# Weight sums on VectorE, a gate stage that stays in PSUM, and a last norm shared by three engines

## The chip, the core and the metric

The kernel runs on one core of one Trainium2 chip. TensorE (PE; its weight loads are PEld) multiplies from SBUF into PSUM, VectorE (DVE), ScalarE (ACT) and GpSimd (POOL) work on tiles in SBUF and PSUM, SyncE (SP) issues the DMA transfers. Every engine works through its own instructions in a fixed order and waits where an operand is not there. The metric is the device time of one execution in microseconds; lower is better.

## The reference

One layer of a hybrid encoder, for 1024 tokens of width 1024, in fp32:

```
x = LN1(alpha*x + 0.5*SwiGLU_1(x))
x = LN2(alpha*x + W_o[ RMS(FoX(x)) || RMS(ShortConv(x)) ])
x = LN3(alpha*x + 0.5*SwiGLU_2(x))
x = LN4(alpha*x + sigmoid(x W_g + b_g) * (p W_p))

SwiGLU(x): gate, up = split(x @ w_in);  return (silu(gate) * up) @ w_out     # hidden width 2816
```

The change touches the output product `... @ w_out` of both SwiGLU blocks and the last line (the gate stage).

## The kernel before

**Precision.** An fp32 product is made from three matmuls of a reduced format: each operand is split into a hi part (a copy by ScalarE, line 123) and a lo part (source minus hi, by VectorE, line 124; both inputs lie in SBUF), and `mm3` (lines 142 to 144) adds hi·hi, lo·hi and hi·lo in PSUM. A block of weights of 128x512 passes through rings of seven hi tiles (`wh`) and seven lo tiles (`wl`); six tiles take loads from HBM (`raw`) and five are for intermediates (`tmp`). There are eight PSUM banks of 128x512.

**Output product (`ffn_out`, called once for each FFN).** The product of hidden activations and w_out is made by a scheme of Strassen and Winograd with seven products of half-size blocks. Each product n = 0 to 6 has eleven steps j; a step splits one tile of hidden activations (`H`, loaded from `h_d`) and one block of weights, and issues 4 token tiles x 3 matmuls of 512 columns. The weights are: b11 (n = 0), t3 = b22 - b12 (n = 1), t2 = t3 + b11, formed in place (n = 2), t4 (n = 3), t1 (n = 4), b21 (n = 5), b22 (n = 6). t3, t2, t4 and t1 are sums of two blocks that GpSimd forms (lines 137 and 417; 44 sums in each FFN). After a product, four banks are evicted into the row tiles `r0` to `r7` by VectorE (line 467: `r += 0.5*ps`); so the residual must be in `r` before. `rest` loads the residual, a quarter (four tiles of 128x512) during each of products 0 to 3, and ScalarE (FFN 1, line 523) or GpSimd (FFN 2, line 976, times the gains) scales it. In FFN 2 a row of biases is added by a matmul with a one-step contraction (line 465: 33 rows, `ones_k`). Rows r0 to r3 are normalised in product 5, r4 to r7 at the end of product 6 (`norm`: statistics on VectorE, the power -0.5 on GpSimd at line 223, the scaling on VectorE).

**Gate stage.** It follows FFN 2 without a break: w_g is split block by block (`w_block`), and the first half of the tokens is multiplied with it for both halves n of the columns; the rows r4 to r7 are transposed (line 207) between the steps. `affine` turns the normalised rows into the residual of the last line (times a gain, plus a bias, on GpSimd, lines 1055 and 1056; 16 operations for four rows). `gate` finishes a bank: bias on VectorE from a broadcast row (line 1028), sigmoid on ScalarE (line 1029), times the projected embedding on GpSimd (line 1030; on VectorE for the last two), and the sum with `r` on VectorE (line 1031), then statistics (line 1036). `finish_out` is the last norm of a row: statistics, power on GpSimd (line 1043), and two operations for each half row on VectorE:

```
        stt = nc.vector.scalar_tensor_tensor
        for n in range(2):
            o = r[t][:, half(n)]
            stt(o, o, mv[:, 0:1], gb4[n], op0=sub, op1=mult)
            stt(o, o, rs, gb4[2 + n], op0=mult, op1=add)
            nc.sync.dma_start(out[tok(t), half(n)], o)
```

**Order.** The kernel is written in a tile framework: its scheduler decides, from its own estimates of time, where an instruction stands on its engine, except where `keep_in_program_order` or, in the change, `issue_after` (not ahead of a given instruction) binds it.

Of the kernel before, what the change touches and what calls it, by code (L numbers as in the profile page):

```python
# [8 lines left out]
F32 = mybir.dt.float32  # L9
# [9 lines left out]
P = 128  # L19
# [6 lines left out]
H = 8  # L26
# [25 lines left out]
def kernel(ctx: ExitStack, tc: tile.TileContext, x, xT, pT, f1_in, f1_out, f2_in,  # L52
# [247 lines left out]
    def ffn_in(w_in, get, early, wait, free, first=None):  # L300
# [77 lines left out]
        up.release()  # L378

    def ffn_out(w_out, init, after0, after1, extra=None):  # L380

# [15 lines left out]
        def h_load(n, j):  # L397
# [41 lines left out]
        for n, (_, get_w, b, (i, nn)) in enumerate(prods):  # L439
# [539 lines left out]
    def row_pair(o, n):  # L979


        a = [temp() for _ in range(n + 1)]
        for i, t in enumerate(a):
            nc.vector.memset(t[0:33], 0.0)
            for q in (0, 32):
                nc.sync.dma_start(t[q:q + 1], rows[3:4, half(i)])
        if n:
            nc.vector.tensor_tensor(a[1][0:33], a[1][0:33], a[0][0:33], op=sub)
        t, l = a[n], temp()
        nc.vector.tensor_scalar(t[0:33], t[0:33], 2 * ALPHA, None, op0=mult)  # L990
        nc.scalar.copy(o[0:33], t[0:33])
# [4 lines left out]
    def after0(r):  # L996
# [25 lines left out]

    def gate(hf, t, ps, c0, w=HB, eng=nc.gpsimd):
# [144 lines left out]
```

## Time and profile before

| | |
|---|---|
| three runs, us | 1951.53, 1954.69, 1953.48 (median 1953.48) |
| profiled execution, us | 1955.81 |
| its span, from the first to the last instruction, us | 1954.0 |
| mean granted TensorE clock | 0.985 |
| busy: TensorE, VectorE, GpSimd, ScalarE | 1874.5, 1442.4, 997.6, 799.8 us |
| FFN 1's output product, about | 442 to 655 us |
| FFN 2's output product, about | 1611 to 1844 us |
| gate stage and end, about | 1815 to 1954 us |

Windows give, for a stretch of time, the busy time of each engine in the order PE, PEld, DVE, ACT, POOL with the number of instructions that started, then TensorE's granted clock as a share of full speed, the share of time in which the DMA engines were busy, and GB/s. Waits name an engine and a line, and after the arrow the instruction whose end released it. Matmuls overlap, so a matmul's listed duration is longer than its share of TensorE's time; the pieces of the chain show that share.

### The profile page before, as it was taken

The numbers are of one execution on the slowest core, as the hardware profiler recorded it, in microseconds if no ns is written. First come the engines' busy times: TensorE is split into PE (matmuls) and PEld (weight loads), VectorE is DVE, ScalarE is ACT, GpSimd is POOL, SyncE is SP. The second block draws the span as 40 slices with busy tenths as digits, with TensorE's granted clock in tenths as the row PEclk, the third lists the DMA queues.
The fourth block names the chain that finished last, engine by engine and source line by source line (L and its number), as shares of the span: only waits on it lengthen the run. The fifth ranks groups of instructions, "written<-read, shape, count | busy, mean of one in ns | idle before, by whom it ended". The sixth has DMA issues, their size and how long they took to land.

```text
span 1954.0 us, 25776 instructions
## 1 busy us (share of the span) xinstructions
PE 1874.5 (96%) x8632; PEld 1540.8 (79%) x8632; DVE 1442.4 (74%) x1999; ACT 799.8 (41%) x1420; POOL 997.6 (51%) x725
## 2 busy tenths in 40 slices
PE   8799999999999989999899999999999999899896
PEld 7688888888788868887688778888888887688685
DVE  7966555548767689976988877976555568987968
ACT  5322333325444553444665526433333334344430
POOL 2787566545550154431841322697565546850673
PEclk9899999999999999999999999999999999999998
DMA  7454323239555533378963123455332249554312
GB/s 238 150 185 163 117 102 119 96 121 379 171 186 178 183 115 119 105 253 273 267 172 91 56 91 118 146 194 178 105 124 93 97 139 365 186 189 152 123 59 98
DMA packets 167938, 307.60 MB, mean 157 GB/s; under 512 B 18503, under 2 KB 26951, under 8 KB 167805
## 3 DMA queue, kind: packets, MB, share of 16 engines
q1 hardware_dynamic: 167804, 305.95, 46.4%
q8 instruction: 68, 1.11, 0.2%
q14 instruction: 66, 0.53, 0.1%
HBM read 221.93 MB, written 83.95 MB: 157 GB/s over the span
## 4 chain that ended last, share of the span: by engine, by line
PE 76%; DVE 12%; issue 5%; DMA 3%; POOL 2%; ACT 1%; SPq 0%; DVEq 0%; ACTq 0%; POOLq 0%
PE ps L143 23%; PE ps L144 22%; PE ps L142 22%; DVE wl L124 4%; DVE tt L137 1%; PE pt L830 1%; PE pt L142 1%; PE pt L143 1%; PE pt L144 1%; PE ps_s L785 1%; PE po L838 1%; PE ps_s L782 1%; DVE S L124 1%; DVE pr L792 1%; PE po L837 1%
## 5 line engine op out<-in xcount | busy, mean ns | idle before, releaser
L142 PE MATMUL ps<-S,wh 128*128 128x512 f32 x896 | 350.8, 392 | 14.0 <-ACT S L123 6.5
L143 PE MATMUL ps<-S,wh 128*128 128x512 f32 x896 | 350.8, 392 | 4.0 <-DVE S L124 4.0
L144 PE MATMUL ps<-S,wl 128*128 128x512 f32 x896 | 350.2, 391 | 0.4 <-DVE wl L124 0.4
L123 ACT CAST wh<-tmp 128x512 fp32r<-128x512 f32 x268 | 164.7, 621 | 355.7 <-PE ps L143 268.5
L124 DVE TENSOR_TENSOR wl<-tmp,wh 128x512 fp32r<-128x512 f32 x268 | 256.8, 959 | 32.4 <-ACT wh L123 32.2
L143 PE MATMUL ps<-wl,wh 128*128 128x512 f32 x616 | 243.3, 395 | 15.1 <-DVE wl L124 15.1
L124 DVE TENSOR_TENSOR wl<-raw,wh 128x512 fp32r<-128x512 f32 x231 | 200.1, 870 | 75.7 <-ACT wh L123 75.4
L123 ACT CAST wh<-raw 128x512 fp32r<-128x512 f32 x239 | 146.6, 621 | 261.7 <-PE ps L143 208.3
L137 POOL TENSOR_TENSOR tmp<-raw 128x512 f32<-128x512 f32 x112 | 159.9, 1428 | 165.2 <-DVE wl L124 106.0
L144 PE MATMUL ps<-wh,wl 128*128 128x512 f32 x616 | 241.1, 391 | 0.0
L142 PE MATMUL ps<-wh 128*128 128x512 f32 x616 | 226.4, 393 | 0.7 <-ACT wh L123 0.7
L137 POOL TENSOR_TENSOR tmp<-raw,tmp 128x512 f32<-128x512 f32 x112 | 158.0, 1411 | 114.4 <-DVE wl L124 54.3
L142 PEld LDWEIGHTS ps<-S,wh 128*128 128x128 f32 x896 | 169.1, 189 | 50.5 <-ACT S L123 7.3
L143 PEld LDWEIGHTS ps<-S,wh 128*128 128x128 f32 x896 | 169.2, 189 | 40.5 <-DVE S L124 5.7
L144 PEld LDWEIGHTS ps<-S,wl 128*128 128x128 f32 x896 | 169.2, 189 | 36.2 <-DVE wl L124 1.1
L343 POOL TENSOR_TENSOR c<-c,sil 128x512 f32<-128x512 f32 x78 | 124.0, 1591 | 74.2 <-DVE c L250 43.3
L143 PEld LDWEIGHTS ps<-wl,wh 128*128 128x128 f32 x616 | 116.2, 189 | 45.8 <-DVE wl L124 22.2
L124 DVE TENSOR_TENSOR wl<-H,wh 128x512 fp32r<-128x512 f32 x154 | 147.4, 957 | 2.3 <-ACT wh L123 2.2
L142 PEld LDWEIGHTS ps<-wh 128*128 128x128 f32 x616 | 115.5, 188 | 25.8 <-ACT wh L123 1.8
L144 PEld LDWEIGHTS ps<-wh,wl 128*128 128x128 f32 x616 | 116.3, 189 | 23.5
L137 POOL TENSOR_TENSOR c<-c 128x512 f32<-128x512 f32 x88 | 128.1, 1460 | 6.7 <-DMA c<-e_d 1.9
L262 DVE TENSOR_TENSOR u<-ps,u 128x512 f32<-128x512 f32 x136 | 92.0, 683 | 47.2 <-PE ps L144 47.1
(299 smaller groups left out, 3988.0 us busy)
## 6 DMA issues: line engine op xcount, KB each, us to landing
raw<-in_f_in SPq DMA_DIRECT2D x216, 256.0 KB
h_d<-c SPq DMA_DIRECT2D x154, 256.0 KB
H<-h_d SPq DMA_DIRECT2D x154, 256.0 KB
raw<-in_f_out SPq DMA_DIRECT2D x132, 256.0 KB
z_d<-r SPq DMA_DIRECT2D x16, 512.0 KB
raw<-in_w_conv_in SPq DMA_DIRECT2D x32, 256.0 KB
r<-z_d SPq DMA_DIRECT2D x32, 256.0 KB
s_d<-s SPq DMA_DIRECT2D x28, 256.0 KB
```

The costliest lines, as they stand in the source:

```text
L123: nc.scalar.copy(h, src)
L124: (eng or nc.vector).tensor_tensor(l, src, h.bitcast(F32), op=sub)
L137: eng.tensor_tensor(t, a, b, op=op)
L142: mm(ps, a[0], b[0], start=first, stop=False, skip_group_check=onto)
L143: mm(ps, a[0], b[1], start=False, stop=False, skip_group_check=onto)
L144: mm(ps, a[1], b[0], start=False, stop=last, skip_group_check=onto)
L262: nc.vector.tensor_tensor(o, ps, u, op=add)
L343: nc.gpsimd.tensor_tensor(c, c, sil.pop((j, i, hf)), op=mult)
L782: mm(st[:, b:b + n], q["QA"][:, tok(t)], q["KA"][:, b:b + n], start=True, stop=False)
L785: mm(st[:, b:b + n], q["QB"][:, tok(t)], q["KB"][:, b:b + n], start=False, stop=True)
L792: nc.vector.tensor_scalar(pr[:, 0:w], pr[:, 0:w], l, None, op0=mult)
L830: nc.tensor.transpose(pv[:, j, t, :], prs[t][:, tok(2 * jp + j)], ident)
```

## The change

1. The sums t3, t2, t4 and t1 go from GpSimd to VectorE. t2, t4 and t1 may not stand ahead of the lo part of the block five steps on in the product before (`done`).
2. The first product's banks are evicted by ScalarE as `r = 0.5*ps`, without a residual. The residual's quarters come in products 1 to 4 in another order; the quarter (1, 0), which comes last, is loaded into a `tmp` tile and added to `r` (FFN 1: one operation on VectorE; FFN 2: a multiplication and an addition on GpSimd, so GpSimd has 20 operations there instead of 16).
3. In `gate`, the bias is a one-step matmul into the bank; sigmoid (ScalarE) and the multiplication (VectorE) work in PSUM, and VectorE adds `r`. The bank is free only after that sum. `row_pair` now also prepares the bias rows.
4. In `finish_out`, ScalarE normalises, VectorE multiplies by the gain, and GpSimd adds the bias (VectorE for the last row).
5. `affine(0)` stands behind the power of the last `norm` on GpSimd.

```diff
     def put(h, l, src, eng=None):
         nc.scalar.copy(h, src)
-        (eng or nc.vector).tensor_tensor(l, src, h.bitcast(F32), op=sub)
+        return (eng or nc.vector).tensor_tensor(l, src, h.bitcast(F32), op=sub)
...
+        def sums(n, j, o, a, b, op):
+            with tc.issue_after(done[n - 1, min(j + 5, NP - 1)]):
+                nc.vector.tensor_tensor(o, a, b, op=op)
+            return o
...
         def w_t3(j):
             b22, b12 = load(w_out[j + NP][:, half(1)]), load(w_out[j][:, half(1)])
-            return tt(nc.gpsimd, b22, b12, sub, lambda: ztile(NP + j))
+            return tt(nc.vector, b22, b12, sub, lambda: ztile(NP + j))
 
         def w_t2(j):
             t = ztile(NP + j)
-            tc.keep_in_program_order(nc.gpsimd.tensor_tensor(t, t, ztile(j), op=add))
-            return t
+            return sums(2, j, t, t, ztile(j), add)
 
         def w_t4(j):
-            return tt(nc.gpsimd, load(w_out[j + NP][:, half(0)]), ztile(NP + j), sub)
+            return sums(3, j, temp(), load(w_out[j + NP][:, half(0)]), ztile(NP + j), sub)
...
-                if n < 4 and j in (1, 3, 5, 7):
+                if n > 0 and n < 5 and j in (1, 3, 5, 7):
                     next(late_init)
...
-                nc.vector.scalar_tensor_tensor(rs, ps[t], 0.5, rs, op0=mult, op1=add)
+                if n == 0:
+                    nc.scalar.activation(rs, ps[t], AF.Copy, scale=0.5)
+                else:
+                    nc.vector.scalar_tensor_tensor(rs, ps[t], 0.5, rs, op0=mult, op1=add)
                 if n == 6:
-                    norm(r[4 + t])
+                    last_norm[0] = norm(r[4 + t])
...
-        for i, nn in ((1, 0), (0, 1), (0, 0), (1, 1)):
+        for i, nn in ((0, 1), (0, 0), (1, 1), (1, 0)):
             for t in range(4 * i, 4 * i + 4):
                 o = r[t][:, half(nn)]
-                tc.keep_in_program_order(nc.sync.dma_start(o, src[tok(t), half(nn)]))
-                yield o, nn
+                z = temp() if (i, nn) == (1, 0) else o
+                tc.keep_in_program_order(nc.sync.dma_start(z, src[tok(t), half(nn)]))
+                yield z, o, nn
...
-        for o, n in rest(r, z_d[1]):
-            tc.keep_in_program_order(nc.gpsimd.tensor_tensor(o, o, gains[n], op=mult))
+        for z, o, n in rest(r, z_d[1]):
+            tc.keep_in_program_order(nc.gpsimd.tensor_tensor(z, z, gains[n], op=mult))
+            if z is not o:
+                tc.keep_in_program_order(nc.gpsimd.tensor_tensor(o, o, z, op=add))
             yield
...
-        pl, c = load(ple_d[tok(row), cs]), temp((P, w))
-        nc.vector.tensor_tensor(c, ps, bg[:, cs], op=add)
-        nc.scalar.activation(c, c, AF.Sigmoid)
-        eng.tensor_tensor(c, c, pl, op=mult)
-        nc.vector.tensor_tensor(r[row][:, cs], r[row][:, cs], c, op=add)
+        pl = load(ple_d[tok(row), cs])
+        mm(ps, ones_k, bg[c0 // HB][:, c0 % HB:c0 % HB + w], start=False, stop=True,
+           skip_group_check=True)
+        nc.scalar.activation(ps, ps, AF.Sigmoid)
+        nc.vector.tensor_tensor(ps, ps, pl, op=mult)
+        nc.vector.tensor_tensor(r[row][:, cs], ps, r[row][:, cs], op=add)
...
-        stt = nc.vector.scalar_tensor_tensor
+        off = small.tile([P, 1], F32, name="off", tag="off")
+        nc.vector.scalar_tensor_tensor(off, mv[:, 0:1], -1.0, rs, op0=mult, op1=mult)
         for n in range(2):
             o = r[t][:, half(n)]
-            stt(o, o, mv[:, 0:1], gb4[n], op0=sub, op1=mult)
-            stt(o, o, rs, gb4[2 + n], op0=mult, op1=add)
+            nc.scalar.activation(o, o, AF.Identity, bias=off, scale=rs)
+            nc.vector.tensor_tensor(o, o, gb4[n], op=mult)
+            eng.tensor_tensor(o, o, gb4[2 + n], op=add)
             nc.sync.dma_start(out[tok(t), half(n)], o)
...
-    affine(0)
+    with tc.issue_after(last_norm[0]):
+        affine(0)
...
     for t in outs:
-        finish_out(t)
+        finish_out(t, nc.vector)
```

**Where instructions stand.** On VectorE, in product 1 of FFN 2, before: lo parts of `H` and of the weights t3 (`T`) take turns.

```order
L124 TENSOR_TENSOR wl_15988<-H_15755,wh_15987 128x512
L124 TENSOR_TENSOR wl_15998<-T_15995,wh_15997 128x512
L124 TENSOR_TENSOR wl_16017<-H_15755,wh_16016 128x512
L124 TENSOR_TENSOR wl_16026<-T_15995,wh_16025 128x512
L124 TENSOR_TENSOR wl_16044<-H_15817,wh_16043 128x512
L124 TENSOR_TENSOR wl_16054<-T_16051,wh_16053 128x512
```

The same place in the change:

```order
L137 TENSOR_TENSOR T_15993<-raw_15989,raw_15991 128x512
L124 TENSOR_TENSOR wl_15932<-T_15937,wh_15931 128x512
L414 TENSOR_TENSOR T_15755<-T_15755,T_15525 128x512
L137 TENSOR_TENSOR T_15993<-raw_16018,raw_16020 128x512
L124 TENSOR_TENSOR wl_15957<-H_15701,wh_15956 128x512
L124 TENSOR_TENSOR wl_15961<-T_15937,wh_15960 128x512
L414 TENSOR_TENSOR T_15821<-T_15821,T_15525 128x512
L124 TENSOR_TENSOR wl_15984<-H_15747,wh_15983 128x512
L137 TENSOR_TENSOR T_16049<-raw_16045,raw_16047 128x512
L124 TENSOR_TENSOR wl_15988<-T_15993,wh_15987 128x512
```

Between the lo parts now stand sums t3 (line 137), which need two loads (`raw`), some steps ahead of their use, and sums t2 for the next product (line 414).

On GpSimd, around the last norm of FFN 2, before (`rs` is the power of `norm`; `gb` the gain and the bias of `affine`):

```order
L137 TENSOR_TENSOR tmp<-raw,T 128x512 x14
L223 TENSOR_TENSOR rs<-rs,mhalf 128x1 x4
L1055 TENSOR_TENSOR r_15489<-r_15489,gb_17608 128x512
L1055 TENSOR_TENSOR r_15490<-r_15490,gb_17608 128x512
...
L1056 TENSOR_TENSOR r_15491<-r_15491,gb_17608 128x512
L1056 TENSOR_TENSOR r_15492<-r_15492,gb_17608 128x512
L223 TENSOR_TENSOR rs<-rs,mhalf 128x1 x4
```

And in the change:

```order
L995 TENSOR_TENSOR tmp<-tmp,gains 128x512
L997 TENSOR_TENSOR r_15500<-r_15500,tmp 128x512
L223 TENSOR_TENSOR rs<-rs,mhalf 128x1 x8
L1081 TENSOR_TENSOR r_15493<-r_15493,gb_17620 128x512
L1081 TENSOR_TENSOR r_15494<-r_15494,gb_17620 128x512
...
L1082 TENSOR_TENSOR r_15493<-r_15493,gb_17620 128x512
L1082 TENSOR_TENSOR r_15494<-r_15494,gb_17620 128x512
```

The sums t4 and t1 (`tmp<-raw,T`) are gone, and the 16 operations of `affine(0)` stand behind all eight powers; all eight multiplications now come ahead of the eight additions.

On VectorE, the end of the program before (`r_15495` and `r_15496` are the last two rows):

```order
L1047 SCALAR_TENSOR_TENSOR r_15495<-r_15495,mv,gb 128x512 x2
L1030 TENSOR_TENSOR tmp<-tmp,raw 128x256
L1048 SCALAR_TENSOR_TENSOR r_15495<-r_15495,rs,gb 128x512 x2
L1031 TENSOR_TENSOR r_15496<-r_15496,tmp 128x256
L1036 BN_STATS st_18248<-r_15496 128x6
L1040 BN_AGGR mv<-st_18248 128x2
L1042 TENSOR_SCALAR rs<-mv 128x1
L1047 SCALAR_TENSOR_TENSOR r_15496<-r_15496,mv,gb 128x512 x2
L1048 SCALAR_TENSOR_TENSOR r_15496<-r_15496,rs,gb 128x512 x2
```

And in the change (the same rows are `r_15499` and `r_15500`):

```order
L1069 SCALAR_TENSOR_TENSOR off<-mv,rs 128x1
L1073 TENSOR_TENSOR r_15499<-r_15499,gb 128x512 x2
L1054 TENSOR_TENSOR ps<-ps,raw 128x256
L1055 TENSOR_TENSOR r_15500<-ps,r_15500 128x256
L1060 BN_STATS st_18271<-r_15500 128x6
L1064 BN_AGGR mv<-st_18271 128x2
L1066 TENSOR_SCALAR rs<-mv 128x1
L1069 SCALAR_TENSOR_TENSOR off<-mv,rs 128x1
L1073 TENSOR_TENSOR r_15500<-r_15500,gb 128x512 x2
L1074 TENSOR_TENSOR r_15500<-r_15500,gb 128x512 x2
```

Ahead of the last row's product, VectorE now has two multiplications of the row before instead of four operations.

## Rows read from the trace of the kernel before

**Rows 1.** The page: busy time by engine (1), and the chain by engine (4).
```profile
PE 1874.5 (96%) x8632; PEld 1540.8 (79%) x8632; DVE 1442.4 (74%) x1999; ACT 799.8 (41%) x1420; POOL 997.6 (51%) x725
...
PE 76%; DVE 12%; issue 5%; DMA 3%; POOL 2%; ACT 1%; SPq 0%; DVEq 0%; ACTq 0%; POOLq 0%
```

**Rows 2.** Window, undisturbed: busy us (x count) of PE, PEld, DVE, ACT, POOL; clock.
```profile
570.00:590.00 20.00, 20.00 (x90) 16.57 (x89) 13.63 (x18) 8.88 (x16) 6.47 (x4) 1.00 0.52 173
```

**Rows 3.** Windows of both output products; columns as in rows 2.
```profile
490.00:510.00 20.00, 19.09 (x84) 15.25 (x84) 19.36 (x15) 8.39 (x15) 20.00 (x13) 1.00 0.58 191
510.00:530.00 20.00, 19.34 (x84) 15.40 (x83) 11.47 (x18) 10.72 (x20) 2.20 (x2) 1.00 0.45 149
...
1650.00:1670.00 20.00, 19.23 (x82) 14.79 (x81) 20.00 (x13) 8.00 (x14) 19.22 (x12) 1.00 0.84 282
1670.00:1690.00 20.00, 16.91 (x69) 12.34 (x68) 20.00 (x16) 5.70 (x10) 20.00 (x13) 1.00 0.51 174
1690.00:1710.00 20.00, 18.56 (x81) 14.67 (x80) 17.86 (x18) 8.00 (x14) 12.91 (x9) 1.00 0.44 145
```

**Rows 4.** Line 124 on VectorE in three stretches: ns min/median/max.
```profile
L124 DVE TENSOR_TENSOR wl<-T,wh x6: 1221/1777/1783, 489.3 to 508.1; 128x512 fp32r<-128x512 f32 x6
...
L124 DVE TENSOR_TENSOR wl<-tmp,wh x8: 668/692/1779, 570.2 to 586.7; 128x512 fp32r<-128x512 f32 x8
...
L124 DVE TENSOR_TENSOR wl<-T,wh x6: 1232/1776/1780, 1670.8 to 1689.0; 128x512 fp32r<-128x512 f32 x6
```

**Rows 5.** Line 467 on VectorE, whole span.
```profile
L467 DVE SCALAR_TENSOR_TENSOR r<-ps,r x56: 665/678/693, 470.1 to 1849.7; 128x512 f32<-128x512 f32 x56
```

**Rows 6.** Pieces of the chain in order of time: start, us, what.
```profile
569.89 0.91 PE ps L142 x4
...
1768.43 1.13 PE ps L465 x4
```

**Rows 7.** Waits, 1590 to 1815 us: us in total, times, longest.
```profile
POOL T L137 <- DMA raw<-in_f_out: 12.5, 2, 11.7
...
PE ps L143 <- DVE wl L124: 5.3, 9, 1.1
```

**Rows 8.** Timeline of GpSimd around the last norm: start, us, work.
```profile
1814.95 6.42 POOL L1055 TENSOR_TENSOR r<-r,gb 128x512 f32<-128x512 f32 x4 [34.48 <-PE ps L207]
...
1834.80 6.80 POOL L1056 TENSOR_TENSOR r<-r,gb 128x512 f32<-128x512 f32 x4
1853.06 4.25 POOL L223 TENSOR_TENSOR rs<-rs,mhalf 128x1 f32<-128x1 f32 x4 [11.45 <-DVE rs L222]
```

**Rows 9.** Windows at the start of the gate stage; columns as in rows 2.
```profile
1825.00:1830.00 5.00, 2.64 (x11) 1.46 (x9) 5.00 (x4) 2.98 (x6) 5.00 (x4) 1.00 0.19 60
1830.00:1835.00 5.00, 0.00 (x0) 0.00 (x0) 5.00 (x4) 3.70 (x7) 5.00 (x4) 0.73 0.43 150
1835.00:1840.00 5.00, 4.56 (x12) 3.61 (x13) 5.00 (x4) 0.33 (x1) 5.00 (x4) 0.59 0.48 159
1840.00:1845.00 5.00, 3.96 (x17) 2.93 (x16) 4.61 (x6) 0.62 (x1) 1.60 (x1) 1.00 0.45 156
```

**Rows 10.** Timelines of TensorE and VectorE, end; the window from 1936 us.
```profile
1935.75 0.28 PE L144 MATMUL ps<-wg,A22l 128*128 128x256 f32 x1
...
1949.08 1.41 DVE L1048 SCALAR_TENSOR_TENSOR r<-r,rs,gb 128x512 f32<-128x512 f32 x2
...
1936.00:1954.00 18.00, 0.03 (x1) 0.00 (x0) 14.36 (x30) 1.46 (x3) 4.14 (x4) 0.56 0.24 88
```

**Rows 11.** Groups of line 976, 1611 to 1844 us: busy, mean ns.
```profile
L976 POOL TENSOR_TENSOR r<-r,gains 128x512 f32<-128x512 f32 x16 | 26.2, 1660 | 3.0 <-ACT gb L494 3.0
```

**Rows 12.** Line 1029 on ScalarE (sigmoid): ns min/median/max.
```profile
L1029 ACT ACTIVATE tmp<-tmp x17: 416/632/634, 1870.7 to 1943.2; 128x512 f32<-128x512 f32 x15, 128x256 f32<-128x256 f32 x2
```

**Rows 13.** Waits, 430 to 660 us.
```profile
POOL T L137 <- DMA raw<-in_f_out: 19.9, 8, 6.0
```

**Rows 14.** Waits, 1815 to 1954 us.
```profile
ACT wg L123 <- DMA raw<-in_w_g: 14.9, 6, 7.9
```

More of the change, by code (lines that the diff above doesn't have):

```diff
@@ L222, in norm @@
         nc.vector.tensor_scalar(rs, mv[:, 1:2], LN_EPS, None, op0=add)
-        nc.gpsimd.tensor_tensor(rs, rs, mhalf[:, 0:1], op=ALU.pow)
+        power = nc.gpsimd.tensor_tensor(rs, rs, mhalf[:, 0:1], op=ALU.pow)
         nc.vector.tensor_scalar(r, r, mv[:, 0:1], rs, op0=sub, op1=mult)
+        return power.ins
     later = []
@@ L378, in ffn_in @@
         up.release()
+    last_norm = [None]
     def ffn_out(w_out, init, after0, after1, extra=None):
@@ L404, in h_load @@
             H[n, j] = t
+        done = {}
+        def sums(n, j, o, a, b, op):
+            with tc.issue_after(done[n - 1, min(j + 5, NP - 1)]):
+                nc.vector.tensor_tensor(o, a, b, op=op)
+            return o
         def w_b11(j):
@@ L412, in w_t3 @@
             b22, b12 = load(w_out[j + NP][:, half(1)]), load(w_out[j][:, half(1)])
-            return tt(nc.gpsimd, b22, b12, sub, lambda: ztile(NP + j))
+            return tt(nc.vector, b22, b12, sub, lambda: ztile(NP + j))
         def w_t2(j):
             t = ztile(NP + j)
-            tc.keep_in_program_order(nc.gpsimd.tensor_tensor(t, t, ztile(j), op=add))
-            return t
+            return sums(2, j, t, t, ztile(j), add)
         def w_t4(j):
-            return tt(nc.gpsimd, load(w_out[j + NP][:, half(0)]), ztile(NP + j), sub)
+            return sums(3, j, temp(), load(w_out[j + NP][:, half(0)]), ztile(NP + j), sub)
         def w_t1(j):
-            return tt(nc.gpsimd, load(w_out[j][:, half(1)]), ztile(j), sub)
+            return sums(4, j, temp(), load(w_out[j][:, half(1)]), ztile(j), sub)
         def w_b21(j):
@@ L447, in ffn_out @@
                     h_load(*fresh.pop(0))
-                h, w = split(H.pop((n, j))), split(get_w(j))
-                if n < 4 and j in (1, 3, 5, 7):
+                h, w = split(H.pop((n, j))), ring()
+                done[n, j] = put(*w, get_w(j)).ins
+                if n > 0 and n < 5 and j in (1, 3, 5, 7):
                     next(late_init)
@@ L513, in rest @@
     def rest(r, src):
-        for i, nn in ((1, 0), (0, 1), (0, 0), (1, 1)):
+        for i, nn in ((0, 1), (0, 0), (1, 1), (1, 0)):
             for t in range(4 * i, 4 * i + 4):
                 o = r[t][:, half(nn)]
-                tc.keep_in_program_order(nc.sync.dma_start(o, src[tok(t), half(nn)]))
-                yield o, nn
+                z = temp() if (i, nn) == (1, 0) else o
+                tc.keep_in_program_order(nc.sync.dma_start(z, src[tok(t), half(nn)]))
+                yield z, o, nn
     def init1(r):
-        for o, _ in rest(r, x):
-            nc.scalar.mul(o, o, ALPHA)
+        for z, o, _ in rest(r, x):
+            if z is o:
+                nc.scalar.mul(o, o, ALPHA)
+            else:
+                nc.vector.scalar_tensor_tensor(o, z, ALPHA, o, op0=mult, op1=add)
             yield
@@ L974, in init2, with row_pair @@
             nc.scalar.mul(gains[n], gains[n], ALPHA)
-        for o, n in rest(r, z_d[1]):
-            tc.keep_in_program_order(nc.gpsimd.tensor_tensor(o, o, gains[n], op=mult))
+        for z, o, n in rest(r, z_d[1]):
+            tc.keep_in_program_order(nc.gpsimd.tensor_tensor(z, z, gains[n], op=mult))
+            if z is not o:
+                tc.keep_in_program_order(nc.gpsimd.tensor_tensor(o, o, z, op=add))
             yield
-    def row_pair(o, n):
-        a = [temp() for _ in range(n + 1)]
+    def row_pair(o, row, n, scale, step):
+        a = [temp() for _ in range(2 if step else 1)]
         for i, t in enumerate(a):
@@ L985, in row_pair @@
             for q in (0, 32):
[L986 to L990, printed above, removed]
+                nc.sync.dma_start(t[q:q + 1], rows[row:row + 1, half(n - i)])
+        t, l = a[0], temp()
+        if step:
+            nc.vector.tensor_tensor(t[0:33], t[0:33], a[1][0:33], op=sub)
+        if scale != 1.0:
+            nc.vector.tensor_scalar(t[0:33], t[0:33], scale, None, op0=mult)
         nc.scalar.copy(o[0:33], t[0:33])
@@ L1002 @@
     r, rA, rB = ffn_out(f2_out, init2, after0, lambda r: None,
-                        [row_pair(extra[n], n) for n in range(2)])
+                        [row_pair(extra[n], 3, n, 2 * ALPHA, n == 1) for n in range(2)])
     gp = pool("gp")
@@ L1036, in gate, with finish_out @@
             nc.vector.bn_stats(sts[row][:, x * m // D, :], r[row][:, x:x + D // m])
-    def finish_out(t):
+    def finish_out(t, eng=nc.gpsimd):
         mv = small.tile([P, 2], F32, name="mv", tag="mv")
@@ L1070 @@
                 X["A22"] = slots((2, 3), "A22h"), slots((14, 15), "A22l")
-                bg = slot(16, "bg", F32, (P, D))
-                nc.sync.dma_start(bg, rows[8].partition_broadcast(P))
+                bg = [row_pair(o, 8, i, 1.0, False) for i, o in enumerate(slots((16,), "bg"))]
             if n == 0 and k >= 4 or n == 1 and k < 4:
@@ L1089 @@
                     mm3(ps, x_blk(1, k, t), b, k == 0, k == KT - 1)
-                gate(1, t, ps, n * HB + q * w, w, nc.vector if w < HB else nc.gpsimd)
+                gate(1, t, ps, n * HB + q * w, w)
             outs.append(t if n else 4 + t)
```

2 lines of the change are left out of this document (1 added, 1 removed).

## The prediction

> **What bounds the kernel now.** I read the page first: TensorE is busy 96% of the span, and of the chain that ended last 76% is TensorE and 12% VectorE [rows 1]. A gain must therefore come from stretches in which TensorE stands still, or from the tail in which it has nothing left to do. The windows find those stretches. An undisturbed one holds 90 matmuls in 20 us, 4.5 per us [rows 2]. With that as the measure I looked for windows with fewer matmuls at a granted clock of 1.00, and asked the waits who was late.
>
> Both output products have such windows: 490 to 530 us holds 84 and 84, and 1650 to 1710 us holds 82, 69 and 81 [rows 3]. In three of those five VectorE is busy 19.4 to 20.0 of 20 us and GpSimd 19.2 to 20.0 us; in the undisturbed window they are busy 13.6 and 6.5. The cause is in the lo parts of the splits (line 124), whose two inputs lie in SBUF: one takes 0.68 to 0.69 us in a quiet stretch, and 1.78 us while GpSimd runs tensor operations [rows 4]. An eviction of the same tile with one input in PSUM took 0.665 to 0.693 us in all 56 cases, those amid GpSimd's work too [rows 5]. A step has twelve matmuls, 12 x 0.227 = 2.72 us [rows 6], and needs two lo parts. At 1.78 us these are 3.5 us, more than the step; at 0.68 us they are 1.4 us. TensorE's waits name just that operation [rows 7].
>
> The gate stage is the third place. From 1814.95 us GpSimd runs 16 affine operations without a break to 1841.6 us, 1.6 to 1.7 us each [rows 8]. VectorE meanwhile needs its lo parts of product 6 and of w_g, is busy all 5 us of each window, and TensorE gets 11, 0, 12 and 17 matmuls where 22.5 would fit [rows 9]. Its granted clock, 1.00 before, is 0.73 and 0.59 in the two middle windows, between its full 2.4 GHz and its lower 1.2 GHz, since it has stood still; it is back at 1.00 from 1840 us. The fourth place is the tail. The last matmul starts at 1935.75 us, VectorE's last operation ends near 1949.8 us, and the span is 1954.0 us: 18 us, of which VectorE is busy 14.4 [rows 10].
>
> **The change, part by part.** *Weight sums to VectorE.* 88 sums leave GpSimd. A sum on VectorE has two SBUF inputs, like a lo part: from below 0.60 us (the pitch: 0.68 less the overlap of neighbours), from above 1.78 us if GpSimd still works [rows 4]. I take 0.60, for in products 1 to 4 little is left on GpSimd. A step then costs VectorE three operations, 1.8 us of 2.72, so it becomes no bound, and TensorE gets back what it loses now:
> FFN 1: (90 - 84) x 2 = 12 matmuls / 4.5 = 2.7 us.
> FFN 2: (90 - 82) + (90 - 69) + (90 - 81) = 38 / 4.5 = 8.4 us [rows 3].
>
> FFN 2 keeps GpSimd work: the 16 multiplications by the gains (1.66 us each [rows 11]) and four new additions. Each can cost VectorE 1.78 - 0.68 = 1.1 us, 22 us for the 20. In products 1 to 4 (44 steps, 120 us) VectorE has 132 x 0.60 = 79 us of lo parts and sums, some 10 us of evictions, and these 22: 111 of 120 us. On average it fits. In product 4, where a multiplication and an addition fall into one step, that step needs 1.8 + 2.2 = 4.0 us against 2.72, and has to live on the ring of seven weight tiles. I hold back 1.5 us for that.
>
> The Trainium skill ("SBUF — State Buffer", section "Who interferes with whom") says that a VectorE instruction with two SBUF inputs contends with a GpSimd instruction that reads SBUF, and that one with at most one SBUF input does not. The 1.78 against 0.68 us, and the unmoved 0.68 us of the evictions, agree with it. The rule speaks against this change as well, since each sum it puts on VectorE is of the kind that contends; by it alone the 20 operations left in FFN 2 would decide, which is rival B.
>
> *First eviction on ScalarE, residual a product later.* Eight evictions leave VectorE for ScalarE, where a tile of 128x512 takes 0.63 us [rows 12]; ScalarE is busy 41% [rows 1] and hides them. Nothing waits for the residual before the norms of products 5 and 6, so its later loads and the four extra VectorE additions in FFN 1 count nothing; uncovered they would be 4 x 0.68 us.
>
> *Affine behind the last norm.* The 16 operations [rows 8] move out from under product 6. The 50 missing matmuls of the four windows (90 - 40 [rows 9]) come back: 50 / 4.5 = 11.1 us. From below, nothing comes back if the weights of the gate are late anyway (rival D).
>
> *Bias by one-step matmuls.* 15 of 512 columns and 2 of 256, on TensorE itself. The rows of line 465 give 1.13 us for four, 0.28 each; the plain pitch is 0.227 [rows 6]. 16 full ones cost 3.6 to 4.5 us; I take 4.0, lost. For it the VectorE addition and GpSimd's multiplication of each tile go. Sigmoid with PSUM as source and destination is not shown; from SBUF it takes 0.632 us [rows 12], a VectorE operation on PSUM 0.678 [rows 5]. I take these. Preparing the bias row adds a few operations on 33 partitions in the middle of the first half, hidden by matmuls.
>
> *Last norm.* Now VectorE does four operations of 0.7 us per token tile at the end. In the change it does two multiplications; ScalarE normalises (0.63 each), GpSimd adds the bias (1.3 to 1.7 each), for the last tile VectorE. Counted from the last matmul: last sigmoid, product, sum, statistics and power about 5.2 us, behind it ScalarE 1.3, then the last multiplication and two additions, 2 to 2.5 us: 8.5 to 9 us. The output transfer takes as long as now (1954.0 - 1949.8 = 4.2 us). Tail: 12.7 instead of 18.0, a gain of 5.3 us (4 to 6).
>
> *Sum:* 2.7 + 8.4 + 11.1 - 4.0 + 5.3 = 23.5 us, less the 1.5 held back: 22.0. The span of 1954.0 us becomes 1932.0; the profiled execution took 1955.81 us, 2.3 more than the median of 1953.48, so I take the gain from the median: **1931.5 us**.
>
> **The rivals.** *A, slower: VectorE stands for the loads of the sums.* GpSimd waited 19.9 us in FFN 1 and 12.5 us in FFN 2 for the weights of the first sums [rows 7, 13]. There this cost nothing, since GpSimd had nothing else to do; on VectorE the lo parts of the running product are queued behind a waiting sum. If all 32.4 us came onto the path the time would be 1931.5 + 32.4 = 1964 us. It decides against the change once more than 22 us of them get through. Against it: the ring of seven weight tiles holds about 3.5 steps, 9 us, of work that is ready, GpSimd's first sums were done before the places where VectorE now needs them, and the waits are in many pieces in FFN 1.
>
> *B: the 20 GpSimd operations left in FFN 2 keep VectorE slow.* If half of the 8.4 us stays lost: 1931.5 + 4.2 = 1936 us. For it: 111 of 120 us leaves little room, and the multiplications come in bunches.
>
> *C: the gate stage gives something back.* The PSUM banks of the first half are now held until the residual is added, and that waits for the affine, which starts behind the norm. In the new order the first tile's addition is the 9th and the last the 12th of the 16 operations; at 1.67 us these end 15 to 20 us behind the norm. TensorE needs the first bank back after six steps of 2.72 us and 16 transposes, about 18 us. If VectorE's adds find the whole 26.7 us in front of them, TensorE stands 8.1 us: 1939.5 us.
>
> *D: the gate stage gives nothing.* ScalarE waited 14.9 us for loads of w_g, 7.9 in one wait [rows 14]. If these, not VectorE, set the start, the 11.1 us stay lost, the bias still costs 4.0, and the tail may keep half its gain: 2.7 + 8.4 - 4.0 + 2.6 - 1.5 = 8.2, 1945 us; with part of B on top it comes within 4 us of now. Against it: those loads were themselves behind VectorE, which frees the tiles that they land in.
>
> **How the numbers follow.** Main case 0.60 (its own range 1926 to 1936), C 0.15, B 0.13, A 0.06, D 0.06. The range 1925 to 1942 holds the main case, B and C and leaves out A, D and a remainder of the rest. A measurement here tells about 0.2%, 3.9 us, from no change. Faster: 0.60 + 0.15 + 0.13 + half of D = 0.91; same: the other half of D, 0.03; slower: A, 0.06.
>
> **What would show it.** In the profile after: no lo part near 1.78 us between 490 and 530 us, and 90 matmuls per 20 us there; 85 or more in each window of FFN 2's products 1 to 4; no 5 us without a matmul before the last norm of FFN 2; TensorE's last matmul about 17 us earlier and a tail of 12 to 13 us. The forecast is wrong if VectorE shows waits for weight loads longer than 9 us, if TensorE shows waits for VectorE's lo parts again in FFN 2, or if a hole between the last norm and the second half of the gate takes the place of the one at 1830 us.

## The result, and the profile after

The changed kernel took 1937.54 us (median of 4 runs, 1934.43 to 1939.2) against 1954.09 us (4 runs, 1951.53 to 1959.63): a ratio of 0.991 with a 95% interval of 0.9885 to 0.9935, a gain of about 17 us where 22 were forecast. The time lies inside the range. The profiled execution has a span of 1935.1 us, 18.9 less than the 1954.0 before.

The page of the changed kernel, busy time by engine and the chain by engine (they answer to [rows 1]):

```profile
PE 1879.9 (97%) x8649; PEld 1543.9 (80%) x8649; DVE 1414.5 (73%) x2079; ACT 815.9 (42%) x1444; POOL 857.1 (44%) x640
...
PE 84%; DVE 7%; DMA 5%; issue 2%; ACT 1%; SPq 1%; POOL 0%; DVEq 0%; POOLq 0%; ACTq 0%
```

VectorE has 80 instructions more than before and is busy 28 us less: part of GpSimd's tensor work beside it went (997.6 to 857.1 us), and with it many of the doubled durations. The windows of both output products and of the start of the gate stage (columns as in [rows 2]; they answer to [rows 3, 9]):

```profile
490.00:510.00 20.00, 20.00 (x90) 16.57 (x89) 16.17 (x27) 11.37 (x21) 0.00 (x0) 1.00 0.50 175
510.00:530.00 20.00, 20.00 (x90) 16.57 (x89) 13.00 (x21) 9.04 (x17) 0.00 (x0) 1.00 0.51 178
1650.00:1670.00 20.00, 20.00 (x90) 16.57 (x89) 18.65 (x26) 8.43 (x15) 4.68 (x3) 1.00 0.71 247
1670.00:1690.00 20.00, 20.00 (x89) 16.54 (x89) 19.26 (x26) 8.72 (x16) 10.25 (x5) 1.00 0.47 164
1690.00:1710.00 20.00, 20.00 (x90) 16.57 (x89) 16.77 (x27) 8.00 (x14) 0.43 (x1) 1.00 0.62 204
...
1820.00:1825.00 5.00, 5.00 (x24) 4.14 (x23) 4.22 (x7) 2.71 (x5) 0.00 (x0) 1.00 0.34 117
1825.00:1830.00 5.00, 5.00 (x24) 4.14 (x23) 4.32 (x8) 2.58 (x5) 0.00 (x0) 1.00 0.30 108
1830.00:1835.00 5.00, 5.00 (x24) 4.14 (x23) 4.64 (x16) 1.05 (x2) 1.99 (x4) 1.00 0.32 107
1835.00:1840.00 5.00, 5.00 (x25) 4.07 (x24) 5.00 (x5) 1.24 (x2) 5.00 (x4) 1.00 0.14 52
```

Where 84, 84, 82, 69 and 81 matmuls stood, there are now 90, 90, 90, 89 and 90. The hole at the start of the gate stage is closed, and TensorE's granted clock is 1.00 in all these windows, its full level of 2.4 GHz. Line 124 on VectorE from 490 to 510 us (ns min/median/max; it answers to [rows 4]):

```profile
L124 DVE TENSOR_TENSOR wl<-H,wh x8: 682/684/691, 489.5 to 508.5; 128x512 fp32r<-128x512 f32 x8
L124 DVE TENSOR_TENSOR wl<-T,wh x7: 684/691/693, 491.0 to 507.9; 128x512 fp32r<-128x512 f32 x7
```

Still, TensorE finishes only 11.7 us earlier, at 1924.35 instead of 1936.03 us. To see where the rest went, I cut each trace at instructions that all kernels share: the first matmul of FFN 1's output product, the first transpose in its product 6, the first one-step matmul of FFN 2 (product 0), the first transpose in FFN 2's product 6, the first transpose of rows r4 to r7, the end of the last matmul, and the end of the span. All times in the table are differences of such starts and ends (us); the last column is the span less the other columns.

| kernel | FFN 1 out to product 6 | FFN 2 products 1 to 5 | product 6, gate start | gate to last matmul | tail | all else |
|---|---|---|---|---|---|---|
| before | 187.6 | 166.1 | 53.4 | 77.7 | 18.0 | 1451.3 |
| after | 185.7 | 158.4 | 42.0 | 85.6 | 10.8 | 1452.7 |
| e1: 128 rows in one-step matmuls | 185.0 | 157.1 | 42.0 | 81.6 | 11.2 | 1452.6 |
| e2: sums on GpSimd | 188.5 | 166.5 | 42.0 | 85.6 | 10.8 | 1448.8 |
| e3: affine not behind the norm | 185.5 | 157.7 | 53.0 | 85.6 | 10.8 | 1451.8 |
| e4: last norm on VectorE | 185.0 | 158.8 | 41.8 | 85.6 | 8.3 | 1450.9 |
| e5: before + sums alone | 185.1 | 160.8 | 53.4 | 77.7 | 18.0 | 1455.0 |
| e6: before + affine alone | 190.9 | 164.8 | 41.8 | 77.6 | 27.7 | 1450.0 |
| e7: after, no gate bias | 185.0 | 159.1 | 42.0 | 77.8 | 12.8 | 1448.4 |
| e8: e1 + e4 | 185.0 | 158.4 | 41.8 | 81.5 | 8.7 | 1453.0 |
| e9: e1 + old norm of the last row | 185.6 | 158.6 | 42.0 | 81.6 | 9.5 | 1449.1 |
| e10: after, old residual order | 185.7 | 159.9 | 42.0 | 85.6 | 11.4 | 1451.9 |

"All else" moves between 1448 and 1455 us without order; most of it is code that no kernel changed. So a total says little about 2 or 3 us. Stages whose code is the same agree to 0.2 us up to the gate's last matmul and to 0.6 us in the tail. The output products spread more: 157.1 to 159.1 us in FFN 2 among kernels that share its sums and residual, and 187.6 against 190.9 us in FFN 1 between the kernel before and e6, whose code is the same there. Every kernel starts 816 matmuls in the FFN 1 stage and 692 in the FFN 2 stage, so these differences are time in which TensorE stands between two of them (in e1, e8 and e9 also the cheaper one-step matmuls). From before to after: 1.9 + 7.8 + 11.4 - 7.9 + 7.2 - 1.5 = 18.9 us.

### The profile page after: what moved, and what is told of

Same layout as the page of the kernel before. It is cut to its first block, busy times and chain, and to the rows that moved or that the text cites. A ratio compares the mean times of both kernels' runs of the same rounds, so it can differ in the third digit from the quotient of the medians.

```text
span 1935.1 us, 25743 instructions
## 1 busy us (share of the span) xinstructions
PE 1879.9 (97%) x8649; PEld 1543.9 (80%) x8649; DVE 1414.5 (73%) x2079; ACT 815.9 (42%) x1444; POOL 857.1 (44%) x640
## 4 chain that ended last, share of the span: by engine, by line
PE 84%; DVE 7%; DMA 5%; issue 2%; ACT 1%; SPq 1%; POOL 0%; DVEq 0%; POOLq 0%; ACTq 0%
PE ps L143 25%; PE ps L142 25%; PE ps L144 25%; DVE wl L124 1%; DVE tt L137 1%; PE pt L849 1%; PE ps L207 1%; DVE pr L811 1%; DMA H<-h_d 1%; PE pt L142 1%; PE pt L143 1%; PE pt L144 1%; PE po L857 1%; DMA T<-in_f_out 1%; DVE m L806 1%
## 5 line engine op out<-in xcount | busy, mean ns | idle before, releaser
L124 DVE TENSOR_TENSOR wl<-tmp,wh 128x512 fp32r<-128x512 f32 x268 | 246.8, 922 | 20.7 <-ACT wh L123 20.5
L142 PE MATMUL ps<-wh 128*128 128x512 f32 x616 | 220.3, 392 | 0.0
L223 POOL TENSOR_TENSOR rs<-rs,mhalf 128x1 f32<-128x1 f32 x24 | 18.1, 795 | 314.5 <-DVE rs L222 253.6
```

What stands on the lines that cost most here:

```text
L124: return (eng or nc.vector).tensor_tensor(l, src, h.bitcast(F32), op=sub)
L142: mm(ps, a[0], b[0], start=first, stop=False, skip_group_check=onto)
```

## The experiments

**e1: the one-step matmuls on 128 rows.** The gate's matmul stage grew by 7.9 us, not by 4.0. The edit:

```diff
-    ones_k = const.tile([33, P], F32R, name="ones_k")
+    ones_k = const.tile([P, P], F32R, name="ones_k")
...
-            nc.vector.memset(t[0:33], 0.0)
+            nc.vector.memset(t, 0.0)
...
-        nc.scalar.copy(o[0:33], t[0:33])
+        nc.scalar.copy(o, t)
...
-        return o[0:33]
+        return o
```

> The changed kernel, with the ones and the bias rows of the one-step matmuls on all 128 partitions (zeros outside the two rows) instead of 33; the products are the same. In the changed kernel's trace a lone one-step matmul in the gate stage takes 0.62 us of TensorE: it starts 0.32 us after the matmul ahead instead of 0.227, takes 0.43, and the matmul behind it 0.33. Theory 1, it is the change of the number of rows, at which the weight load is not made ahead of time: with 128 rows each costs the plain 0.227 us, 17 of them 3.9 instead of some 8.2 us, and the gate stage from the first transpose to the last matmul becomes 4 to 4.5 us shorter than 85.6 us; with the 8 of FFN 2 some 5 us in all, about 1932.5 us. Theory 2, a one-step matmul is dear whatever its rows, since a bank's accumulation ends in it and another's begins: nothing changes, 1937.5 us.

1931.56 us (ratio 0.9873, 0.9858 to 0.9888), and 81.6 us instead of 85.6 in the stage: theory 1. The two timelines show it. In the changed kernel, matmuls and weight loads (PEld) around one bias (start, duration, work):

```profile
1880.17 0.39 PE L143 MATMUL ps<-wl,A22h 128*128 128x512 f32 x1
1880.39 0.39 PE L144 MATMUL ps<-wh,A22l 128*128 128x512 f32 x1
1880.71 0.50 PE L1051 MATMUL ps<-bg,ones_k 33*128 33x512 f32 x1
1881.14 0.50 PE L142 MATMUL ps<-wg,A21h 128*128 128x512 f32 x1
1881.47 0.39 PE L143 MATMUL ps<-wg,A21h 128*128 128x512 f32 x1
```

```profile
1880.17 0.19 PEld L144 LDWEIGHTS ps<-wh,A22l 128*128 128x128 f32 x1
1880.71 0.18 PEld L1051 LDWEIGHTS ps<-bg,ones_k 33*128 33x128 f32 x1 [0.35 <-issue]
1881.14 0.19 PEld L142 LDWEIGHTS ps<-wg,A21h 128*128 128x128 f32 x1 [0.25 <-issue]
1881.25 0.19 PEld L143 LDWEIGHTS ps<-wg,A21h 128*128 128x128 f32 x1
```

And in e1, matmuls and weight loads at the same place:

```profile
1883.18 0.40 PE L144 MATMUL ps<-wh,A22l 128*128 128x512 f32 x1
1883.42 0.40 PE L1051 MATMUL ps<-bg,ones_k 128*128 128x512 f32 x1
1883.65 0.39 PE L142 MATMUL ps<-wg,A21h 128*128 128x512 f32 x1
```

```profile
1883.19 0.19 PEld L1051 LDWEIGHTS ps<-bg,ones_k 128*128 128x128 f32 x1
1883.42 0.19 PEld L142 LDWEIGHTS ps<-wg,A21h 128*128 128x128 f32 x1
```

The load for line 144 starts at 1880.17, 0.22 us ahead of its matmul. The load of 33 rows starts with its own matmul, at 1880.71, and so does the next load of 128 rows, at 1881.14. In e1 both loads start 0.23 us ahead of their matmuls. The three steps from 1880.39 to 1881.47 take 1.08 us, where two of the plain pitch, without the bias, would take 0.45: the bias costs 0.62 us, 0.40 beyond its own 0.227. With 128 rows the bias costs 0.23 to 0.24. The Trainium skill ("TensorE: Matmul & The Clock Gate", section "Why this matters for your kernels") says that a single matmul of 32 rows takes the time of one of 128. The load itself, 0.18 against 0.19 us, agrees; in a stream of 128-row matmuls the lone one of 33 rows does not, and the measurement decides.

**e2: the sums back on GpSimd.**

```diff
-            return tt(nc.vector, b22, b12, sub, lambda: ztile(NP + j))
+            return tt(nc.gpsimd, b22, b12, sub, lambda: ztile(NP + j))
...
-            return sums(2, j, t, t, ztile(j), add)
+            tc.keep_in_program_order(nc.gpsimd.tensor_tensor(t, t, ztile(j), op=add))
+            return t
```

(and the same for t4 and t1.)

> The changed kernel with the four sums back on GpSimd (line 137 and the two others), all else as changed. Theory 1, the sums on GpSimd are what doubles the lo parts: FFN 2's products 1 to 4 lose about 7.8 us again and FFN 1's about 2, lo parts at 1.78 us between 490 and 510 us; about 1947 us. Rival, it was the later residual and the first eviction on ScalarE that gave the gain in FFN 2: little comes back, about 1938 us.

1944.92 us (ratio 0.9944, 0.9929 to 0.9959). FFN 2's products went back to 166.5 us, FFN 1's stage to 188.5; the three columns of the gate did not move by 0.1 us. Line 124 on VectorE, 490 to 510 us, and the window from 1670 us:

```profile
L124 DVE TENSOR_TENSOR wl<-H,wh x6: 674/1774/1779, 489.4 to 508.2; 128x512 fp32r<-128x512 f32 x6
L124 DVE TENSOR_TENSOR wl<-T,wh x5: 1256/1775/1783, 491.1 to 506.5; 128x512 fp32r<-128x512 f32 x5
```

```profile
1670.00:1690.00 20.00, 16.95 (x70) 12.31 (x69) 20.00 (x16) 6.84 (x12) 20.00 (x13) 1.00 0.38 131
```

The doubled lo parts and the missing matmuls are both back: the sums on GpSimd were their cause.

**e3: affine(0) where the scheduler puts it.**

```diff
-    with tc.issue_after(last_norm[0]):
-        affine(0)
+    affine(0)
```

> The changed kernel without the rule that affine(0) stands behind the last norm's power; the scheduler then puts the 16 operations ahead of it again. Theory 1, their place under product 6 cost the 11 us at the start of the gate stage: lo parts at 1.78 us and a hole of some 8 us near 1815 to 1830 us, about 1947 us, less what earlier affine operations give back behind it. Rival, the hole came from the loads of w_g and closed for another reason, the earlier sums: no hole, about 1937 us.

1944.14 us (ratio 0.9935, 0.9919 to 0.9952). The stage has 53.0 us instead of 42.0, and the hole is back at the same place of the program (windows of e3):

```profile
1815.00:1820.00 5.00, 2.73 (x12) 1.58 (x10) 5.00 (x4) 3.06 (x6) 5.00 (x4) 0.98 0.20 64
1820.00:1825.00 5.00, 0.00 (x0) 0.00 (x0) 5.00 (x4) 3.67 (x7) 5.00 (x4) 0.50 0.45 148
1825.00:1830.00 5.00, 4.50 (x11) 3.58 (x12) 5.00 (x4) 0.36 (x1) 5.00 (x4) 0.50 0.18 60
```

GpSimd and VectorE are busy 5 of 5 us again. ScalarE's waits for the loads of w_g, on which rival D rested [rows 14], follow the affine too. In the waits of the changed kernel, 1795 to 1870 us (us in total, times, longest):

```profile
ACT wg L123 <- DMA raw<-in_w_g: 1.1, 2, 0.7
```

And in e3:

```profile
ACT wg L123 <- DMA raw<-in_w_g: 14.6, 6, 7.7
```

A load can start when VectorE's lo part has freed the tile it lands in. The DMA queue's own waits for the lo parts of w_g in that stretch, in the changed kernel and then in e3:

```profile
SPq L116 <- DVE wg L124: 6.8, 9, 1.3
```

```profile
SPq L116 <- DVE wg L124: 16.1, 9, 3.0
```

So the loads are late because VectorE is. Behind the hole, 85.6 and 10.8 us are those of the changed kernel: affine's later place gives nothing back there.

**e4: the last norm on VectorE again.**

```diff
-            nc.scalar.activation(o, o, AF.Identity, bias=off, scale=rs)
-            nc.vector.tensor_tensor(o, o, gb4[n], op=mult)
-            eng.tensor_tensor(o, o, gb4[2 + n], op=add)
+            stt(o, o, mv[:, 0:1], gb4[n], op0=sub, op1=mult)
+            stt(o, o, rs, gb4[2 + n], op0=mult, op1=add)
```

> The changed kernel with the last norm of every row as before: two operations for each half row on VectorE, nothing on ScalarE and GpSimd but the power. The tail behind the last matmul fell from 18.0 to 10.75 us. Theory 1, this came from the shorter gate work of each bank (no bias addition and no trip through GpSimd), and the split norm is a longer chain for the last row: the tail becomes 1.5 to 2.5 us shorter still, about 1935.5 us. Rival, the split norm itself made the tail shorter, by taking VectorE's four operations of row 6 out of the way of row 7: without it the tail grows by 3 to 7 us, 1940 to 1944 us.

1934.06 us (ratio 0.9891, 0.9872 to 0.991); the total alone does not tell it from 0.991, the tail does: 8.3 us instead of 10.8. VectorE at the end of the changed kernel:

```profile
1927.15 0.15 DVE L1066 TENSOR_SCALAR rs<-mv 128x1 f32<-128x1 f32 x1
1928.44 0.16 DVE L1069 SCALAR_TENSOR_TENSOR off<-mv,rs 128x1 f32<-128x1 f32 x1 [1.13 <-POOL rs L1067]
1929.48 1.40 DVE L1073 TENSOR_TENSOR r<-r,gb 128x512 f32<-128x512 f32 x2 [0.88 <-ACT r L1072]
1930.79 1.29 DVE L1074 TENSOR_TENSOR r<-r,gb 128x512 f32<-128x512 f32 x2
```

And in e4:

```profile
1924.59 0.15 DVE L1066 TENSOR_SCALAR rs<-mv 128x1 f32<-128x1 f32 x1
1924.66 1.41 DVE L1071 SCALAR_TENSOR_TENSOR r<-r,mv,gb 128x512 f32<-128x512 f32 x2
1925.99 1.41 DVE L1072 SCALAR_TENSOR_TENSOR r<-r,rs,gb 128x512 f32<-128x512 f32 x2
```

From `rs` to the end 4.9 us in the one, 2.8 in the other. The old form subtracts the mean and multiplies while GpSimd works out the power; the new one can do nothing until the power is there, waits 1.13 us for it and 0.88 for ScalarE. The split norm thus costs 2.5 us, and the shorter tail is left to part 3. That is by elimination: parts 1 and 5 alone leave tails of 18.0 and 27.7 us (e5, e6), undoing part 2 leaves 11.4 (e10), and no run has part 3 alone.

**e5 and e6: two parts alone on the kernel before.** e5 has part 1 only (the sums, with `done`), e6 part 5 only (`issue_after` around `affine(0)`); the edits are those of the change.

> The kernel before with the four sums on VectorE and nothing else. Theory 1, the parts act in different stretches and add: FFN 2's output product up to the start of product 6 becomes 7.5 us shorter (166.1 to 158.5 us) and the rest stays as before: 53.4, 77.7 and 18.0 us; about 1945 to 1946 us. Rival, with the multiplications by the gains in products 0 to 3 and VectorE's evictions still there, VectorE has no room for the sums: 3 us or less, about 1951 us.

1950.97 us (ratio 0.9983, 0.9972 to 0.9995). FFN 2's products gain 5.3 of the 7.8 us, FFN 1 2.5; "all else" is 3.7 us longer in this profile. Neither theory's number: the sums do most of their work alone, but not all. From 1660 to 1700 us 84 and 81 matmuls start in 20 us where the changed kernel has about 90, and there the multiplications by the gains run beside VectorE; added up, TensorE's matmuls from 1672 to 1685 us start 3.0 us late (windows of e5):

```profile
1660.00:1680.00 20.00, 19.12 (x84) 15.49 (x83) 19.84 (x28) 8.11 (x15) 10.04 (x5) 1.00 0.74 259
1680.00:1700.00 20.00, 18.73 (x81) 14.85 (x80) 17.07 (x23) 7.96 (x14) 6.11 (x4) 1.00 0.58 195
```

> The kernel before with affine(0) behind the last norm's power and nothing else. Theory 1, the start of the gate stage (first transpose of product 6 to the first of the gate) becomes 11 us shorter, 53.4 to 42 us, and the rest stays: about 1943 us. Rival, what moves runs into GpSimd's multiplications of the gate, which are then queued behind 32 affine operations, so that banks or the last rows come late: the hole comes back behind the norm or the tail grows, and the time is 1946 to 1953 us.

1952.91 us (ratio 0.9991, 0.998 to 1.0002): no change that can be measured. The stage shrinks to 41.8 us as in the changed kernel, and the tail grows by 9.7 us: the rival. Windows of e6 show why:

```profile
1860.00:1880.00 20.00, 20.00 (x98) 16.60 (x97) 7.44 (x8) 8.19 (x13) 20.00 (x16) 1.00 0.09 27
1880.00:1900.00 20.00, 20.00 (x89) 16.55 (x89) 14.32 (x17) 3.10 (x5) 20.00 (x15) 1.00 0.14 47
1900.00:1920.00 20.00, 20.00 (x93) 16.68 (x92) 20.00 (x32) 1.27 (x2) 12.66 (x10) 1.00 0.36 131
1920.00:1940.00 20.00, 5.18 (x44) 4.98 (x42) 19.11 (x31) 2.71 (x5) 7.94 (x7) 0.71 0.19 67
```

From 1860 to 1900 us GpSimd is never free, with affine operations and the gate's multiplications in turn, and VectorE waits 11.7 us for those products. What it could not do then it does later: TensorE is done at 1925.2 us, VectorE has a backlog until 1949.3, 1.2 us ahead of where it ended before. The old gate is bound by GpSimd and then by VectorE; TensorE's 11 us earlier only make the tail longer.

**e7: no gate bias.**

```diff
-        mm(ps, ones_k, bg[c0 // HB][:, c0 % HB:c0 % HB + w], start=False, stop=True,
-           skip_group_check=True)
```

> The changed kernel without the 17 one-step matmuls of the gate, so the gate's bias is left out of the result. From the first transpose to the last matmul 85.6 us were measured with them on 33 rows, 81.6 on 128 rows, 77.65 in the kernel before. If they are all that was added there: 77.4 to 77.8 us, and the tail some 0.3 us shorter. If the banks that are now held until the residual is added cost TensorE something besides: 78.5 us or more.

One run, 1926.84 us; the stage has 77.8 us, so the 17 matmuls are all that was added and holding the banks costs nothing. The tail is 2.0 us longer, not shorter. GpSimd at the end of e7:

```profile
1914.85 2.97 POOL L1072 TENSOR_TENSOR r<-r,gb 128x512 f32<-128x512 f32 x2 [2.44 <-DVE r L1071]
1917.78 0.54 POOL L1065 TENSOR_TENSOR rs<-rs,mhalf 128x1 f32<-128x1 f32 x1
```

The last power is ready to go at 1915.5 us, when `rs` is there, and starts at 1917.78, behind row 6's two bias additions. In the changed kernel this queue costs 0.6 us (1927.30 to 1927.86).

**e8 and e9: towards a faster version.** e8 joins e1 and e4. e9 joins e1 with the old norm for the last row alone.

> The changed kernel with both corrections that the runs point to: one-step matmuls on 128 rows, and the last norm of all rows on VectorE as before. The two lie in different stretches (first transpose to last matmul, and the tail), so they should add: gate stage 81.6 us, tail 8.3 us, 2.5 us less than with the padding alone: about 1929 us. Rival: TensorE's earlier end finds VectorE's four operations of each row still queued, and the tail is 10 us or more: about 1931.5 us, as with the padding alone.

> The changed kernel with one-step matmuls on 128 rows, and the last norm as before for the last row only; the other seven rows keep the split norm. If the longer chain of the split norm counts for the last row alone, the tail is 8.3 to 8.9 us, as with the old norm on all rows: about 1929 us. If GpSimd's two additions for row 6 ahead of the last power, and VectorE's two multiplications, hold the last row up, it is 0.5 us more than with the old norm on all rows.

e8: 1930.15 us (ratio 0.9879, 0.9857 to 0.9901), tail 8.7 us. e9: 1929.06 us (0.9872, 0.9855 to 0.9888), tail 9.5 us: row 6's additions start at 1917.78 us and hold the last power until 1920.72, though its input is there at 1920.15. e8 is as expected by stages. e9 missed its first theory's 8.3 to 8.9 us: its tail is 0.8 us longer than e8's, as the second theory has it, and the last power waits behind row 6's additions. By total, e1, e8 and e9 cannot be told apart, and all lie below the changed kernel's median.

**e10: part 2 undone.**

```diff
-                if n > 0 and n < 5 and j in (1, 3, 5, 7):
+                if n < 4 and j in (1, 3, 5, 7):
...
-                if n == 0:
-                    nc.scalar.activation(rs, ps[t], AF.Copy, scale=0.5)
-                else:
-                    nc.vector.scalar_tensor_tensor(rs, ps[t], 0.5, rs, op0=mult, op1=add)
+                nc.vector.scalar_tensor_tensor(rs, ps[t], 0.5, rs, op0=mult, op1=add)
...
-        for i, nn in ((0, 1), (0, 0), (1, 1), (1, 0)):
+        for i, nn in ((1, 0), (0, 1), (0, 0), (1, 1)):
```

(and every residual quarter loaded straight into `r`.)

> The changed kernel with part 2 undone: the residual in products 0 to 3 in the old order, no temporary tile, all evictions on VectorE. With the sums alone on the kernel before, FFN 2 from its first one-step matmul to product 6 took 160.8 us against 158.4 in the changed kernel and 166.1 before, with 3 us of gaps left near 1670 to 1690 us. Theory 1, these are the multiplications by the gains beside the sums t3 and t2: with part 2 undone the stretch is 160 to 161.5 us again, 2 to 3 us more than in the changed kernel, about 1940 us; part 2 is then worth that much, which the prediction counted as nothing. Rival, the difference lies elsewhere: 158 to 159 us, about 1937.5 us.

1937.79 us (ratio 0.9908, 0.9891 to 0.9924), as the changed kernel. The stage has 159.9 us against 158.4, between the two forecasts and just short of theory 1's. The matmul starts show theory 1's mechanism all the same: in e10 they are 2.1 us late in all, every bit of it from 1674 to 1682 us, where lo parts beside the multiplications take up to 1.78 us; in the changed kernel they are on time there and 0.7 us late in product 4. So part 2 is worth 1.5 us in this pair; against the 157.7 to 159.1 us of all that share the new order and the 33 rows it is 0.8 to 2.2.

## Why the prediction was right, and where its sizes were off

The direction, the places and the range held; of the signs, TensorE's end (11.7 us earlier, not about 17) and the tail (10.8 us, not 12 to 13) were missed. The sum's terms against the stages:

| term | forecast, us | measured, us |
|---|---|---|
| sums, FFN 1 | 2.7 | 1.9 (1.9 to 2.6 in e1, e3 to e5 and e7 to e10); 5.2 against e6, which has the old sums |
| sums, FFN 2 | 8.4 | 7.8; 8.1 between the changed kernel and e2 |
| affine behind the norm | 11.1 | 11.4; 11.0 by e3 |
| bias matmuls | -4.0 | -7.9 |
| tail | 5.3 | 7.2 |
| held back for product 4 | -1.5 | about -0.7, already inside the 7.8 of FFN 2 |
| all else | no term | -1.5, within its spread |

**The sums.** The step "at 1.78 us two lo parts are more than a step" held: e2 brings back the doubled duration and the lost matmuls. Rival A is refuted: VectorE waited 1.0 us for loads of the sums in FFN 1, none in FFN 2. Rival B came, but small. From 1650 to 1710 us 90, 89 and 90 matmuls start beside the multiplications, yet in product 4, where the additions run, 87:

```profile
1730.00:1750.00 20.00, 19.84 (x87) 15.83 (x86) 17.44 (x28) 8.52 (x16) 8.52 (x4) 1.00 0.50 165
```

Sums on VectorE wait for a `tmp` tile that GpSimd's additions free (waits from 1590 to 1815 us):

```profile
DVE tmp L414 <- POOL r L997: 3.7, 2, 2.6
```

The forecast expected the loss in this product, from doubled durations; it put 1.5 us on it, and matmuls start 0.7 us late there. By the letter of its signs TensorE does wait for lo parts again in FFN 2, 0.7 us in three waits where there were 5.3 in nine [rows 7]. Without part 2, e5 and e10 lose 3.0 and 2.1 us to the multiplications instead; the forecast counted that part as nothing.

**The bias was the step that failed in size.** "16 full ones cost 3.6 to 4.5 us" took the price from the rows of line 465 [rows 6]. Those are four in a row, and most of the gate's stand alone. Two changes of the row count are paid per group, and a group of one has nobody to share them. The piece of the chain for four ends with them and leaves out the 0.43 us that the next matmul takes:

```profile
1769.56 0.43 PE ps L142
```

So even a group costs about 1.13 + 0.43 - 0.23 = 1.33 us, 0.33 apiece. Eight in two groups and nine alone make 8 x 0.33 + 9 x 0.62 = 8.2 us, close to the 7.9 measured (two of the nine have 256 columns and cost less). e1 shows the cause: the rows, not the one step.

**The tail was too small, and for a wrong reason.** The forecast put the gain down to the norm shared by three engines. e4 shows that this costs 2.5 us; part 3 earns the gain. Some of it is bought with the bias: without those 17 matmuls TensorE is done earlier, and the tail is 12.8 us (e7). That the total came this near is thus partly luck: the bias is 3.9 us worse than forecast and the tail 1.9 better, and the two hang together. I also read 1949.8 us as VectorE's end; its last operation, two from 1949.08 in 1.41 us [rows 10], ends at 1950.5, and the output transfer behind it takes 3.5 us, 3.0 after.

**The affine** held in size, but the sum treats the parts as independent, and e6 shows that they are not: in the old gate stage the same 11.5 us came out as 9.7 us more tail. Nor does the new gate stage gain alone: e3 takes 53.0 + 85.6 + 10.8 = 149.4 us from product 6 to the end, the kernel before 149.1. Only both together make it 138.4. Rival C did not come: TensorE has no hole behind the norm, and e7 finds no price for the held banks. (The 8.1 us of its working does not follow: 26.7 less about 18 is 8.7.) Nor did D: the hole stayed shut.

**What stays open.** TensorE's last matmul came 11.7 us earlier, not the 17 of the forecast, for the bias and "all else". The latter differs by up to 7 us between profiles; no experiment looked for its cause. FFN 1's gain has no firm size either: with the old sums its stage took 187.6, 188.5 and 190.9 us in three kernels. Whether e9 beats e1 in the total isn't settled.

## What to carry to other kernels

A gain on TensorE is worth only what the engines behind it can follow: before you add up stages, ask for each whether the next one is bound by another engine. Price an instruction in the place where it will stand; a row in which it comes in groups does not show what one alone costs its neighbours. A norm whose first half needs no power is best done while the power is under way, at least for the last row.

## What was not expected of the hardware

A matmul of 33 rows between matmuls of 128 rows costs 0.62 us at full clock, one of 128 rows 0.23 to 0.24. In the trace neither the weight load of the 33 rows nor the next one starts ahead of its matmul; with 128 rows both do. Padding with zeros to 128 rows made the gate's stage, with 17 of them, 4.0 to 4.1 us shorter in each of e1, e8 and e9. For the eight in FFN 2 the stage's times show no gain beyond their spread: 157.1, 158.4 and 158.6 us with it, 157.7 to 159.1 us without.
